# Survey loads on ACT's queue, a bias folded into a stored residual, and one unit's operand sums moved, in a one-layer encoder

## The chip, the cores and the metric

One core of a Trainium2 chip runs the whole kernel. Its engines are TensorE (PE, with PEld for weight loads), VectorE (DVE), ScalarE (ACT), GpSimd (POOL) and SyncE (SP); each runs its own instructions strictly in order, and instructions wait on semaphores. Transfers are carried out by 16 DMA engines and are started by an instruction in some engine's stream: here in SP's, but for one on POOL. Such an instruction can wait too, and everything behind it in the same stream then waits with it. The metric is device time in microseconds (us), median of several runs.

## The reference

A single post-norm encoder layer on x of 1024 tokens by 1024 features, float32, with 256 memory tokens. Cut to what matters:

```python
h = layer_norm(x, ln_in_w, ln_in_b)
h = layer_norm(ALPHA * h + hybrid_mixer(h, ...), ln1_w, ln1_b)        # mLSTM + neighbourhood attention, w_mix_out
h = layer_norm(ALPHA * h + memory_xattn(h, mem, w_xq, w_xkv, w_xo, b_xo), ln2_w, ln2_b)
h = layer_norm(ALPHA * h + conv_ffn(h, w_up, ..., w_down, b_down), ln3_w, ln3_b)

def memory_xattn(x, mem, w_q, w_kv, w_o, b_o):
    ...                                   # 4 heads of 256, softmax over 256 memory tokens
    return o @ w_o + b_o

def conv_ffn(x, w_up, b_up, w_dw, b_dw, w_down, b_down):
    h = x @ w_up + b_up                   # 1024 -> 2 * 2816
    h = depthwise_conv3(h, w_dw) + b_dw   # along the tokens
    g, u = split(h)
    return (gelu(g) * u) @ w_down + b_down
```

## The kernel before

Tokens are handled in eight tiles of 128 (`tt`). Each product is made from three matmuls (`mm3`, lines L217 to L219) of operands that were split into a high and a low part: a copy on ACT and a subtraction on DVE or POOL (`split`, `wload`, `split16`, L126/L127, L189/L190, L222/L223). The float16 splits need a power-of-two scale for each weight matrix, and that scale needs a bound on the matrix's entries. The **survey** finds it: `survey_gen` loads a matrix tile by tile into the buffers `sv` (two of them) and reduces each tile into one column of `sums`, on ACT by a sum of absolute values (L205) or, for column numbers in `BYMAX` (16 to 19), on DVE by a maximum (L203). `scale_of` later turns columns of `sums` into a scale. There are two surveys:

- the first, in the token-chunk stage: 11 tiles of `w_down`, 4 of `w_xo`, 4 of `w_xq` (1 MB each). Its next tile is asked for after a token chunk, inside `tc.issue_after(d.ins)`, which puts the load on SP behind that chunk's store `d` of the buffer `ev` (three buffers, L323 to L330);
- the second, in the stages of the mixer's output projection and of the cross-attention: 44 half-tiles of `w_up` (512 KB each), asked for in `after1` (one for each token tile) and in `attn` (one for each token tile, head and half), the rest by `run(survey)`. Its column numbers 16 to 19 fall into `BYMAX` too.

Stages, in order: input norm and token chunks (`tok_chunk`, PE tile `tk`, weight pieces of `w_tok`); column products (`cl`); mLSTM (`ml_gen`); neighbourhood attention (`na_gen`) with the output projection of the first half as filler; output projection of the second half (`out_half`), whose `after1` makes norm 1 (`ln_tile`), stores the normed tile `r` to the DRAM scratch `h1_d` (L930) and, three tiles later (`LAG`), transposes it into the float16 operands h1 (`to_T16`); query projection (`xq_gen`, PE tiles `xq` and `fill`); cross-attention (`attn`: scores `S`, softmax `P`, transposed `PT`, output `pv`) mixed with the query projection's second part and then with the cross output projection (`out_d`, PE tiles `od` and `out`); the feed-forward in 22 units (`Units`) of 128 columns; the down projection (`dn`).

`out_d` reads the residual back from `h1_d`: `load_r` (L1093) loads a tile into one of four buffers `r` and adds the bias row b_xo, already divided by ALPHA, on POOL (L1094). Norm 2 follows, with its statistics on DVE (L230 to L234), a power on POOL (L235), scale and shift on ACT, DVE and POOL (L241 to L243). Then `to_B` transposes the tile (PE, L989) and prepares the feed-forward's operands: even token tiles give B11 and B21, odd ones T1 to T4 and B22 (L998 to L1010).

A feed-forward unit `v` is one 128x2048 piece of `w_up` with four blocks A11, A12, A21, A22 in a buffer `ur` (two of them, loaded by `Units.load`, L1155). `Units.prep(v)` makes four sums S1 to S4 of the blocks on POOL (L1171 to L1174) into two buffers `wraw`, splits the A blocks from `ur`, then splits the S sums; it yields between these steps. `to_B` uses the same two `wraw` buffers for T1 to T4. Seven products `prod` make a unit: A11 with B11 and A12 with B21 come first and need no T operand; for units 0 and 1 they are issued before the loop over the units begins. `prep(0)` stands ahead of the last four tiles of `out_d`, `prep(1)` after nine steps of them (three tiles).

The written order is not the order on the engines. The program is traced as a whole, and an instruction scheduler with a simulated time line then chooses each engine's order: it starts what is ready when an engine is free, from far ahead in the program too. `mix` and `tc.issue_after` are the means by which the code holds something back: the instructions in such a block come after a named one on its engine.

Of the kernel before, what the change touches and what calls it, by code (L numbers as in the profile page):

```python
# [17 lines left out]
D = 1024  # L18
# [38 lines left out]
def encoder(ctx, tc, I, out):  # L57
# [134 lines left out]
    BYMAX = range(16, 20)  # L192

    def survey_gen(pool, src):

        for ap, i in src:
            shape = list(ap.shape)
            t = pool.tile(shape, F32, name="sv", tag="sv", bufs=2)
            S.dma_start(t, ap)
            if len(shape) > 2:  # L200
                t = t.rearrange("p a c -> p (a c)")
            if i in BYMAX:
                V.tensor_reduce(sums[:, i:i + 1], t, axis=mybir.AxisListType.X, op=OP.max, apply_absolute_value=True)  # L203
            else:
                A.activation(t, t, AF.Abs, accum_out=sums[:, i:i + 1])  # L205
            yield
# [61 lines left out]
    with ExitStack() as ca:  # L268

        yml = None  # L270
        with ExitStack() as cm:
# [19 lines left out]
            with ExitStack() as c1:  # L291
# [4 lines left out]
                    (I["w_xq"][2 * i:2 * i + 2].rearrange("i p k c -> p i (k c)"), 16 + i) for i in range(4)])  # L296
# [10 lines left out]
                def tok_chunk(c, tt, w):  # L307
# [13 lines left out]
                    else:  # L321
# [3 lines left out]
                        if c < 4:  # L325
                            d = S.dma_start(nv_d[tt * 128:(tt + 1) * 128, j:j + 256], e)
                        else:
                            A.activation(e, e, AF.Sigmoid)
                            G.tensor_tensor(e, e, mlw[:, j:j + 256], OP.mult)
                            d = S.dma_start(mo_d[tt * 128:(tt + 1) * 128, j:j + 256], e)  # L330
                        return d
# [33 lines left out]
                for c in range(2, 6):  # L365
                    w = [ws.get(2 * c), ws.get(2 * c + 1)]
                    for tt in range(NT):
                        d = tok_chunk(c, tt, w)
                        if tt % 2 == 0 or c > 3:
                            with tc.issue_after(d.ins):  # L370
                                next(survey, None)
# [521 lines left out]
    with ExitStack() as cb_:  # L893
# [12 lines left out]
        with ExitStack() as cB:  # L906
# [50 lines left out]
            for i in range(XQ0):  # L957
                if i > 0:
                    t_, r_ = rq.pop(0)
                    to_T16(r_, h1, t_, s1)  # L960
# [51 lines left out]
        with ExitStack() as cC:  # L1012
# [61 lines left out]
            bxo = vec(2, "b_xo")  # L1074
            V.tensor_scalar(bxo, bxo, 1.0 / ALPHA, None, op0=OP.mult)
# [14 lines left out]
            def load_r(tt):  # L1090
                if tt < NT:
                    rs[tt] = rt.tile([128, D], F32, name="r", tag="r", bufs=4)
                    S.dma_start(rs[tt], h1_d[tt * 128:(tt + 1) * 128, :])  # L1093
                    G.tensor_tensor(rs[tt], rs[tt], bxo, OP.add)  # L1094
# [51 lines left out]
        class Units:  # L1146
# [16 lines left out]
            def prep(self, v):  # L1163
# [4 lines left out]
                A21, A11, A12, A22 = (raw[:, i * 512:i * 512 + 512] for i in range(4))  # L1168
                s12, s34 = (wp.tile([128, WP], F32, name="wraw", tag="wraw", bufs=2)[:, :1024] for i in range(2))
# [6 lines left out]
                ah, sh_, al, sl = self.home(v)  # L1176
                k4 = lambda h, l, i: tuple(t[:, i * 512:i * 512 + 512].rearrange("p (k c) -> p k c", k=4) for t in (h, l))
                u = {"A11": k4(ah, al, 0), "A12": k4(ah, al, 1), "A22": k4(ah, al, 2)}
                for i in range(4):
                    u[f"S{i + 1}"] = k4(sh_, sl, i)  # L1180
                self.got[v] = u
                split16(ah, al, raw[:, 512:], su)
                yield
# [37 lines left out]
        with ExitStack() as cE:  # L1221
# [303 lines left out]
```

## Time and profile before

| | |
|---|---|
| time, median of 3 runs | 1627.49 us (1625.42 to 1632.18) |
| profiled execution | 1627.17 us, span 1625.5 us |
| mean granted TensorE clock | 0.969 |
| busy: PE, DVE, ACT, POOL | 1503.0, 973.4, 753.2, 544.6 us |
| moved by DMA | 226.69 MB, mean 139 GB/s |
| second survey's loads (`sv`<-`w_up`) | 44, from 636.1 to 796.6 us |

In the lines of the profile, L12 is line 12 of the kernel; an instruction is named engine, line, operation, tile written <- tiles read (buffer numbers left out), and its shape. In an order of time each row begins with the start and the duration in us; "[5.19 <-DVE ev L323]" says that the engine had been idle 5.19 us before it, and what released it. SPq is SP's stream of transfer issues; its rows with several issues ("x3") include waits between them. A row of the chain gives start, length and what was on the chain. A row of the waits gives who waited for whom, us in total, times, and the longest. Slices are 40 equal parts of the span, with digits for the busy share in tenths. PE's busy time is that of pipelined matmuls: whether PE is held up is read from its gaps and from the clock beside them.

### The profile page before, as it was taken

The numbers are of one execution on the slowest core, as the hardware profiler recorded it, in microseconds if no ns is written. First come the engines' busy times: TensorE is split into PE (matmuls) and PEld (weight loads), VectorE is DVE, ScalarE is ACT, GpSimd is POOL, SyncE is SP. The second block draws the span as 40 slices with busy tenths as digits, with TensorE's granted clock in tenths as the row PEclk, the third lists the DMA queues.
The fourth block names the chain that finished last, engine by engine and source line by source line (L and its number), as shares of the span: only waits on it lengthen the run. The fifth ranks groups of instructions, "written<-read, shape, count | busy, mean of one in ns | idle before, by whom it ended". The sixth has DMA issues, their size and how long they took to land.

```text
span 1625.5 us, 21513 instructions
## 1 busy us (share of the span) xinstructions
PE 1503.0 (92%) x8112; PEld 975.5 (60%) x8112; DVE 973.4 (60%) x1719; ACT 753.2 (46%) x1258; POOL 544.6 (34%) x372
## 2 busy tenths in 40 slices
PE   6998999999888989797789968999999999999997
PEld 5998888889777878644345533444444444444443
DVE  7411611237578885767566786887777676835333
ACT  3335201225555765656654444656665655622111
POOL 5414222114457761322002546454345410010133
PEclk9999999999999999898989978999999999999999
DMA  8278511266556325777631313222222232741112
GB/s 299 91 270 299 172 52 59 97 169 177 161 163 214 132 79 187 254 261 255 220 130 39 114 68 107 84 98 91 99 83 78 91 130 78 281 146 53 62 55 78
DMA packets 80377, 226.69 MB, mean 139 GB/s; under 512 B 7824, under 2 KB 26512, under 8 KB 76048
## 3 DMA queue, kind: packets, MB, share of 16 engines
q1 hardware_dynamic: 80128, 224.82, 40.3%
q8 instruction: 64, 1.05, 0.3%
q0 software_dynamic: 144, 0.49, 0.2%
q14 instruction: 41, 0.34, 0.1%
HBM read 182.71 MB, written 43.06 MB: 139 GB/s over the span
## 4 chain that ended last, share of the span: by engine, by line
PE 59%; DMA 12%; DVE 9%; ACT 6%; POOL 5%; issue 4%; SPq 0%; POOLq 0%; ACTq 0%; DVEq 0%
PE z L217 7%; PE z L218 7%; PE z L219 7%; PE dn L218 4%; PE dn L219 4%; PE dn L217 4%; DMA sv<-in_w_up_dram 4%; PE cl L217 4%; PE cl L219 4%; PE cl L218 4%; DMA whi<-mrow 2%; DMA mo<-ev 1%; ACT sv L205 1%; DMA r<-h 1%; PE o L863 1%
## 5 line engine op out<-in xcount | busy, mean ns | idle before, releaser
L127 POOL TENSOR_TENSOR wlo<-wraw,whi 128x1024 fp32r<-128x1024 f32 (+1 forms) x36 | 86.8, 2416 | 193.6 <-ACT whi L126 184.2
L190 DVE SCALAR_TENSOR_TENSOR wlo<-wraw,sc,whi 128x1024 f16<-128x1024 f32 x67 | 87.8, 1319 | 83.8 <-ACT whi L189 83.6
L217 PE MATMUL dn<-whi,yp 128*128 128x512 f16 x336 | 127.2, 379 | 0.0
L218 PE MATMUL dn<-wlo,yp 128*128 128x512 f16 x336 | 127.2, 379 | 0.0
L219 PE MATMUL dn<-whi,yp 128*128 128x512 f16 x336 | 126.9, 379 | 0.0
L189 ACT ACTIVATE whi<-wraw,sc 128x1024 f16<-128x1024 f32 x67 | 75.8, 1144 | 105.4 <-PE dn L219 46.3
L235 POOL TENSOR_TENSOR lnrs<-lnrs,mhalf 128x1 f32<-128x1 f32 x32 | 26.3, 822 | 283.9 <-DVE lnrs L234 161.6
L126 ACT ACTIVATE whi<-wraw 128x1024 fp32r<-128x1024 f32 (+1 forms) x48 | 50.4, 1056 | 121.8 <-PE cl L218 75.4
L205 ACT ACTIVATE sv<-sv 128x1024 f32<-128x1024 f32 (+1 forms) x55 | 70.9, 1289 | 71.8 <-DMA sv<-in_w_down_dram 38.3
L1173 POOL TENSOR_TENSOR wraw<-ur 128x512 f32<-128x512 f32 x22 | 41.2, 1873 | 156.1 <-DVE wlo L190 73.6
L243 POOL TENSOR_TENSOR r<-r,vec 128x1024 f32<-128x1024 f32 x22 | 51.8, 2356 | 77.5 <-DVE r L242 69.4
L1434 POOL TENSOR_TENSOR r<-r,vec 128x1024 f32<-128x1024 f32 x8 | 19.0, 2376 | 158.2 <-ACT r L1433 158.2
L1250 DVE SCALAR_TENSOR_TENSOR cbuf<-C,wdw,cbuf 128x1024 f32<-128x1024 f32 x44 | 70.7, 1607 | 1.1
L217 PEld LDWEIGHTS <-whi 128*128 128x128 f16 x364 | 36.3, 100 | 56.5 <-issue 16.5
L1249 DVE SCALAR_TENSOR_TENSOR cbuf<-C,wdw,cbuf 128x1024 f32<-128x1024 f32 x44 | 63.7, 1448 | 7.7 <-ACT cbuf L1248 6.7
L218 PEld LDWEIGHTS <-whi 128*128 128x128 f16 x364 | 36.2, 99 | 47.7 <-issue 7.7
L219 PEld LDWEIGHTS <-wlo 128*128 128x128 f16 x364 | 36.1, 99 | 45.1 <-issue 3.6
L217 PE MATMUL tk<-whi,X2h 128*128 128x256 f32 (+1 forms) x192 | 56.2, 292 | 6.5 <-DVE ev L323 5.2
L1248 ACT ACTIVATE cbuf<-C,bdw,wdw 128x1024 f32<-128x1024 f32 x44 | 54.4, 1236 | 12.2 <-DVE C L1286 11.4
L219 PEld LDWEIGHTS <-yp 128*128 128x128 f16 x352 | 34.4, 98 | 41.5
L217 PEld LDWEIGHTS <-yp 128*128 128x128 f16 x352 | 34.4, 98 | 41.5
L218 PEld LDWEIGHTS <-yp 128*128 128x128 f16 x352 | 34.4, 98 | 41.4
(444 smaller groups left out, 4850.9 us busy)
## 6 DMA issues: line engine op xcount, KB each, us to landing
sv<-in_w_up_dram SPq DMA_DIRECT2D x44, 512.0 KB
ur<-in_w_up_dram SPq DMA_DIRECT2D x22, 1024.0 KB
r<-h SPq DMA_DIRECT2D x23, 512.0 KB
sv<-in_w_down_dram SPq DMA_DIRECT2D x11, 1024.0 KB
y<-cbuf SPq DMA_DIRECT2D x22, 512.0 KB
ur<-y SPq DMA_DIRECT2D x11, 1024.0 KB
wraw<-in_w_down_dram SPq DMA_DIRECT2D x22, 512.0 KB
wraw<-in_w_col_dram SPq DMA_DIRECT2D x16, 512.0 KB
```

The source lines that it names most:

```text
L126: A.activation(hi[:, :n], r3, AF.Copy)
L127: (eng or G).tensor_tensor(lo[:, :n], r3, hi[:, :n].bitcast(F32), OP.subtract)
L189: A.activation(hi, src, AF.Copy, scale=s)
L190: V.scalar_tensor_tensor(lo, src, s, hi, op0=OP.mult, op1=OP.subtract)
L205: A.activation(t, t, AF.Abs, accum_out=sums[:, i:i + 1])
L217: T.matmul(ps, lh, rh, start=first, stop=False, skip_group_check=skip)
L218: T.matmul(ps, lh, rl, start=False, stop=False, skip_group_check=skip)
L219: return T.matmul(ps, ll, rh, start=False, stop=last, skip_group_check=skip)
L243: G.tensor_tensor(r, r, b_t, OP.add)
L1248: A.activation(c, C[:, 1:SEQ + 1], AF.Identity, scale=wdw[:, 1, j:j + 1], bias=bdw[:, j:j + 1])
L1249: V.scalar_tensor_tensor(c, C[:, 0:SEQ], wdw[:, 0, j:j + 1], c, op0=OP.mult, op1=OP.add)
L1250: V.scalar_tensor_tensor(c, C[:, 2:SEQ + 2], wdw[:, 2, j:j + 1], c, op0=OP.mult, op1=OP.add)
```

## The change

Three edits go together.

1. `survey_gen` issues its loads from ACT. It starts with two loads; then, for each tile, it makes the sum and issues the next load right behind it. The `issue_after` around the first survey is gone. Which columns are reduced on DVE is now an argument: 16 to 19 in the first survey, none in the second.
2. The bias b_xo is loaded before the output projection's second half. The new `to_h1` transposes a tile, then adds the bias in place on POOL, then stores it to `h1_d`; it takes the place of the transpose alone, three tiles behind the norm, and the earlier store is gone. `load_r` only loads, into one of five buffers.
3. `prep` gets the argument `early`, with which the split of the A blocks comes ahead of the S sums. Unit 1 is prepared that way: its A split after six steps of `out_d`, its S sums and their splits in the loop over the units. Unit 2 is loaded right behind `prep(0)`, and in the loop `units.load(v + 3)` comes after the sums of unit `v + 2`.

```diff
-    BYMAX = range(16, 20)
-    def survey_gen(pool, src):
-        for ap, i in src:
-            shape = list(ap.shape)
-            t = pool.tile(shape, F32, name="sv", tag="sv", bufs=2)
-            S.dma_start(t, ap)
...
-            if i in BYMAX:
+    def survey_gen(pool, src, bymax=()):
+        q = []
+        def load():
+            if src:
+                ap, i = src.pop(0)
+                t = pool.tile(list(ap.shape), F32, name="sv", tag="sv", bufs=2)
+                A.dma_start(t, ap)
+                q.append((t if len(ap.shape) == 2 else t.rearrange("p a c -> p (a c)"), i))
+        load()
+        load()
+        yield
+        while q:
+            t, i = q.pop(0)
+            if i in bymax:
                 V.tensor_reduce(sums[:, i:i + 1], t, axis=mybir.AxisListType.X, op=OP.max, apply_absolute_value=True)
             else:
                 A.activation(t, t, AF.Abs, accum_out=sums[:, i:i + 1])
+            load()
             yield
...
-                        d = tok_chunk(c, tt, w)
+                        tok_chunk(c, tt, w)
                         if tt % 2 == 0 or c > 3:
-                            with tc.issue_after(d.ins):
-                                next(survey, None)
+                            next(survey, None)
...
+            bxo = vec(2, "b_xo")
+            V.tensor_scalar(bxo, bxo, 1.0 / ALPHA, None, op0=OP.mult)
+            def to_h1(tt, r):
+                to_T16(r, h1, tt, s1)
+                G.tensor_tensor(r, r, bxo, OP.add)
+                S.dma_start(h1_d[tt * 128:(tt + 1) * 128, :], r)
             def after1(tt, r):
                 holds.append(ln_tile(r, lw, lb, small, hold=holds[-1] if holds else None))
-                S.dma_start(h1_d[tt * 128:(tt + 1) * 128, :], r)
                 next(survey, None)
                 rq.append((tt, r))
                 if len(rq) > LAG:
-                    t_, r_ = rq.pop(0)
-                    to_T16(r_, h1, t_, s1)
+                    to_h1(*rq.pop(0))
...
-                    rs[tt] = rt.tile([128, D], F32, name="r", tag="r", bufs=4)
+                    rs[tt] = rt.tile([128, D], F32, name="r", tag="r", bufs=5)
                     S.dma_start(rs[tt], h1_d[tt * 128:(tt + 1) * 128, :])
-                    G.tensor_tensor(rs[tt], rs[tt], bxo, OP.add)
...
+                if early:
+                    split16(ah, al, raw[:, 512:], su)
+                    yield
                 s12, s34 = (wp.tile([128, WP], F32, name="wraw", tag="wraw", bufs=2)[:, :1024] for i in range(2))
...
-                split16(ah, al, raw[:, 512:], su)
-                yield
+                if not early:
+                    split16(ah, al, raw[:, 512:], su)
+                    yield
...
         run(units.prep(0))
+        units.load(2)
         out_d2 = out_d(range(4, NT), "out", 1)
-        for _ in range(9):
+        for _ in range(6):
             next(out_d2)
-        run(units.prep(1))
-        units.load(2)
+        prep1 = units.prep(1, True)
+        next(prep1)
         run(out_d2)
...
             for v in range(NFF):
-                units.load(v + 3)
+                if v == 0:
+                    run(prep1)
                 pr = units.prep(v + 2)
                 next(pr, None)
+                units.load(v + 3)
```

More of the change, by code (lines that the diff above doesn't have):

```diff
@@ L190, in split16 @@
         V.scalar_tensor_tensor(lo, src, s, hi, op0=OP.mult, op1=OP.subtract)
-    BYMAX = range(16, 20)
-    def survey_gen(pool, src):
-        for ap, i in src:
-            shape = list(ap.shape)
-            t = pool.tile(shape, F32, name="sv", tag="sv", bufs=2)
-            S.dma_start(t, ap)
-            if len(shape) > 2:
-                t = t.rearrange("p a c -> p (a c)")
-            if i in BYMAX:
+    def survey_gen(pool, src, bymax=()):
[12 more added lines that the diff above has]
+            if i in bymax:
                 V.tensor_reduce(sums[:, i:i + 1], t, axis=mybir.AxisListType.X, op=OP.max, apply_absolute_value=True)
@@ L295, in encoder @@
                     (I["w_xo"][256 * i:256 * i + 256].rearrange("(a p) c -> p a c", a=2), 33 + i) for i in range(4)] + [
-                    (I["w_xq"][2 * i:2 * i + 2].rearrange("i p k c -> p i (k c)"), 16 + i) for i in range(4)])
+                    (I["w_xq"][2 * i:2 * i + 2].rearrange("i p k c -> p i (k c)"), 16 + i) for i in range(4)], range(16, 20))
                 ones = smallA.tile([128, 128], F32, name="ones")
@@ L325, in tok_chunk @@
                         if c < 4:
-                            d = S.dma_start(nv_d[tt * 128:(tt + 1) * 128, j:j + 256], e)
+                            S.dma_start(nv_d[tt * 128:(tt + 1) * 128, j:j + 256], e)
                         else:
@@ L329, in tok_chunk @@
                             G.tensor_tensor(e, e, mlw[:, j:j + 256], OP.mult)
-                            d = S.dma_start(mo_d[tt * 128:(tt + 1) * 128, j:j + 256], e)
-                        return d
+                            S.dma_start(mo_d[tt * 128:(tt + 1) * 128, j:j + 256], e)
                 xs = {}
@@ L958, in encoder @@
                 if i > 0:
-                    t_, r_ = rq.pop(0)
-                    to_T16(r_, h1, t_, s1)
+                    to_h1(*rq.pop(0))
                 next(xg)
@@ L1073, in encoder @@
             alx, epx = inx[:, 1:2], inx[:, 2:3]
-            bxo = vec(2, "b_xo")
-            V.tensor_scalar(bxo, bxo, 1.0 / ALPHA, None, op0=OP.mult)
             lw, lb = vec(0, "ln2_w"), vec(1, "ln2_b")
@@ L1161, in home, with prep @@
                 return homes[i]
-            def prep(self, v):
+            def prep(self, v, early=False):
                 if v >= NFF:
@@ L1168, in prep @@
                 A21, A11, A12, A22 = (raw[:, i * 512:i * 512 + 512] for i in range(4))
+                ah, sh_, al, sl = self.home(v)
+                k4 = lambda h, l, i: tuple(t[:, i * 512:i * 512 + 512].rearrange("p (k c) -> p k c", k=4) for t in (h, l))
+                u = {"A11": k4(ah, al, 0), "A12": k4(ah, al, 1), "A22": k4(ah, al, 2)}
+                for i in range(4):
+                    u[f"S{i + 1}"] = k4(sh_, sl, i)
+                self.got[v] = u
+                if early:
+                    split16(ah, al, raw[:, 512:], su)
+                    yield
                 s12, s34 = (wp.tile([128, WP], F32, name="wraw", tag="wraw", bufs=2)[:, :1024] for i in range(2))
@@ L1175, in prep @@
                 yield
[L1176 to L1181, printed above, removed]
-                split16(ah, al, raw[:, 512:], su)
-                yield
+                if not early:
+                    split16(ah, al, raw[:, 512:], su)
+                    yield
                 split16(sh_[:, :1024], sl[:, :1024], s12, su)
```

## The prediction

> **What bounds the kernel now.** I read the page's busy shares and slices first, then the table of stretches, then the chain and the waits, and went into the order of time only where TensorE (PE) idles. The table's columns are the stretch, its length, busy time (and count) of PE, PEld, DVE, ACT, POOL, then the granted clock, the DMA share and GB/s.
>
> ```profile
> PE 1503.0 (92%) x8112; PEld 975.5 (60%) x8112; DVE 973.4 (60%) x1719; ACT 753.2 (46%) x1258; POOL 544.6 (34%) x372
> PE   6998999999888989797789968999999999999997
> q1 hardware_dynamic: 80128, 224.82, 40.3%
> ...
> 0.00:40.00 40.00, 25.75 (x172) 23.18 (x173) 31.29 (x69) 14.47 (x17) 20.70 (x22) 1.00 0.82 304
> 156.00:164.00 8.00, 2.17 (x19) 1.75 (x17) 2.15 (x10) 2.74 (x5) 0.00 (x0) 0.75 0.98 324
> 164.00:180.00 16.00, 15.93 (x103) 15.32 (x104) 14.49 (x28) 3.89 (x7) 4.47 (x5) 0.81 0.73 248
> 640.00:840.00 200.00, 163.92 (x780) 95.75 (x779) 130.49 (x240) 122.60 (x213) 32.58 (x20) 0.90 0.69 237
> 955.00:1000.00 45.00, 25.09 (x90) 11.76 (x90) 36.40 (x40) 19.39 (x28) 26.00 (x23) 0.70 0.20 73
> 1000.00:1600.00 600.00, 598.95 (x2778) 271.82 (x2777) 388.30 (x364) 288.73 (x313) 182.44 (x96) 1.00 0.29 102
> ```
>
> From 1000 to 1600 us PE is full (598.95 of 600) at the full clock: nothing done there can show. The change can pay or cost only where PE has holes: the start, 156 to 180, 640 to 840 (36 us idle, clock 0.90), and 955 to 1000 (20 us idle, clock 0.70). The one dynamic hardware queue, q1, carries everything that SP issues; no row has a load issued by ACT.
>
> ```profile
> PE 59%; DMA 12%; DVE 9%; ACT 6%; POOL 5%; issue 4%; SPq 0%; POOLq 0%; ACTq 0%; DVEq 0%
> ...
> SPq L199 <- ACT sv L205: 71.4, 34, 7.1
> ...
> ACT sv L205 <- DMA sv<-in_w_up_dram: 27.1, 20, 3.7
> ```
>
> SP stood 71.4 us, 34 times, at the survey's load (L199) until ACT had summed the tile whose buffer it takes (L205); whatever SP had behind it stood too. ACT in turn stood 27.1 us for the survey's loads.
>
> **First survey (w_down, w_xo, w_xq).** Gain side:
>
> ```profile
> 154.63 2.64 SPq L330 DMA_DIRECT2D mo<-ev  x3
> 157.37 6.89 SPq L199 DMA_DIRECT2D sv<-in_w_xq_dram  x2
> ...
> 154.63 8.78 DMA mo<-ev
> ...
> 163.49 0.42 DVE L323 TENSOR_TENSOR ev<-tk,btok 128x256 f32<-128x256 f32 x1 [3.45 <-DMA mo<-ev]
> ...
> 163.97 0.58 PE L217 MATMUL tk<-whi,X2h 128*128 128x256 f32 x1 [5.19 <-DVE ev L323]
> ```
>
> A store of `ev` took 8.78 us among survey loads; DVE had no free `ev`, so PE had no free bank and idled 5.19 us. The stretch 156 to 164 lost 5.8 us and the next 16 us ran at 0.81 of the clock, 3.0 us more: 8.9 us. With the loads out of SP's queue the store no longer stands behind them. I take 9 gained; the ends are 0 (the store stays slow, because the DMA engines are 0.98 busy there) and 9.
>
> Cost side: the `issue_after` that held the loads behind SP's stores is gone. (The last row is from a tile's view: count, min/median/max ns, first and last start, forms.)
>
> ```profile
> 1.20 0.55 DVE L429 MEMSET cx<- 64x256 f32 x2
> ...
> 80.19 0.42 SPq L199 DMA_DIRECT2D sv<-in_w_down_dram  x1
> ...
> 10.71 1.11 ACT L126 ACTIVATE whi<-wraw 128x1088 fp32r<-128x1088 f32 x1 [8.62 <-DMA wraw<-in_w_tok_dram]
> ...
> L205 ACT ACTIVATE sv<-sv x55: 1043/1057/1918, 86.9 to 803.5; 128x1024 f32<-128x1024 f32 x40, 128x2048 f32<-128x2048 f32 x15
> ```
>
> The memset of `cx` is written far behind the token chunks and ran at 1.20 us: the order made for an engine takes whatever is ready. The first two survey loads wait for nothing, ACT has nothing else until 10.71, so I expect them at about 1 us instead of 80.19, with the sums following as tiles land. Two tiles are 2.1 MB, at the 304 GB/s of the first 40 us 6.9 us for whatever they delay, and there PE waits for x, the norm's vectors and the first weights. Two further tiles fit into the 18% of those 40 us in which the DMA engines are free. In pairs, 6.9 us to land and twice 1.9 us to sum, about 7 tiles come in 40 us: 24 us. I take 7 lost, near the lower end, since ACT's queue also holds evictions that wait for PE, and every such wait holds back the next survey load; ends 0 and 24.
>
> **Second survey (w_up, 44 tiles), 640 to 804 us.** The tile's view again, the chain, ACT and PE in order of time.
>
> ```profile
> L199 SPq DMA_DIRECT2D sv<-in_w_up_dram x44: 327/328/1167, 636.1 to 796.6; - x44
> L199 SPq DMA_DIRECT2D sv<-in_w_down_dram x11: 328/385/431, 80.2 to 138.7; - x11
> L203 DVE TENSOR_REDUCE sums<-sv x8: 1170/1743/2286, 168.6 to 713.3; 128x1 f32<-128x2048 f32 x4, 128x1 f32<-128x1024 f32 x4
> ...
> 768.97 5.49 DMA sv<-in_w_up_dram
> ...
> 774.54 1.06 ACT L205 ACTIVATE sv<-sv 128x1024 f32<-128x1024 f32 x1 [2.82 <-DMA sv<-in_w_up_dram]
> ...
> 778.48 0.59 PE L217 MATMUL pv<-PTh,vh 128*128 128x512 f16 x1 [5.36 <-ACT PTh L189]
> ```
>
> An issue on ACT has no row; the nearest is 0.33 us on SP. 44 of them are 14.5 us in ACT's queue, behind which stand its exponentials, splits and norms. The four tiles with numbers 16 to 19 also leave DVE (`bymax` is now empty here): 4.7 us off DVE, 4 x 1.06 = 4.2 us onto ACT. So ACT gets 19 us more in a stretch where it is busy 122.60 of 200. Cover: its 77 idle us; where the cover is gone (attention, whose softmax goes through ACT) up to 19 reach the path. For this SP's 71.4 us vanish, so w_xq, w_xo and K/V loads no longer queue behind sums; at best half of PE's 36 idle us, 18. But the hole at 778.48 stays: the load went at 768.97, as soon as its buffer was free, landed 5.49 us later, and ACT stood in order with the attention's copies behind it. Issuing it from ACT changes nothing there. The value between -18 and +19 I set at 0, because both rows are real and neither is nearer.
>
> Here the Trainium skill (DMA: Bandwidth & Descriptors) speaks on both sides. Its section "Issuing engines are not separate DMA queues" says that loads started by several engines run on the same 16 DMA engines, interleaved, and that a second issuer saves only issue time; by it both surveys gain nothing in transfer, which is the third rival below. Its section "Queues, rings and completion order" says that each issuer has a ring of its own and the engines alternate between rings packet by packet; by it the store at 154.63 would overtake the survey loads. No run here shows two rings yet.
>
> **Bias into the stored residual.**
>
> ```profile
> 951.01 2.35 POOL L1094 TENSOR_TENSOR r<-r,vec 128x1024 f32<-128x1024 f32 x1 [3.01 <-DMA r<-h]
> 953.31 0.55 POOL L235 TENSOR_TENSOR lnrs<-lnrs,mhalf 128x1 f32<-128x1 f32 x1
> ...
> 953.90 0.21 DVE L240 TENSOR_SCALAR lnrs<-lnmv,lnrs 128x1 f32<-128x1 f32 x1 [3.37 <-POOL lnrs L235]
> ...
> 959.12 1.12 PE L989 MATMUL tp<-ident,r 128*128 128x128 f32 x4 [3.98 <-POOL r L243]
> ```
>
> Eight adds on POOL leave the output projection for the stage before, and `load_r` gets a fifth buffer. On the path it is one add: DVE's statistics were out by 950.53 (953.90 - 3.37), POOL's power of them stood behind the add until 953.31, and PE's transposes wait for that norm. 953.31 - 950.53 = 2.8 us gained, ends 0 and 2.8. The eight adds (8 x 2.35 = 19 us) go to where POOL is busy 32.58 of 200 us; a norm's power may stand behind one there, up to 2.35 us once. The stores of h1, now after the transposes and the add, are read back one stage later. A tile of `r` comes free some 5 us later; with 7 buffers only the eighth load notices, up to 3 us. I cost these at 0. Loading b_xo earlier is one 512 KB load off the path.
>
> **Second unit's sums later.**
>
> ```profile
> 982.90 1.29 POOL L1174 TENSOR_TENSOR wraw<-ur,wraw 128x512 f32<-128x512 f32 x1
> ...
> 984.21 0.33 SPq L1155 DMA_DIRECT2D ur<-in_w_up_dram  x1
> ...
> 989.25 1.57 ACT L189 ACTIVATE whi<-ur,sc 128x1536 f16<-128x1536 f32 x1 [2.73 <-DMA ur<-in_w_up_dram]
> ...
> 986.80 0.38 PE L218 MATMUL z<-Bh,unitA 128*128 128x512 f16 x1
> 987.02 0.38 PE L219 MATMUL z<-Bh,unitA 128*128 128x512 f16 x1
> 991.91 0.38 PE L217 MATMUL z<-TX1l,unitYh 128*128 128x512 f16 x1 [4.51 <-ACT TX1l L1009]
> 994.29 0.58 PE L218 MATMUL z<-TX1l,unitYh 128*128 128x512 f16 x1 [1.78 <-DVE TX1l L1010]
> ...
> 999.36 0.50 PE L219 MATMUL z<-TX1l,wlo 128*128 128x512 f16 x1
> ```
>
> Unit 1's last sum (982.90) freed the raw buffer, SP loaded unit 3 into it at 984.21, and ACT had that unit's split in its order ahead of the last token tile's T operands: it idled 2.73 us for the load and spent 1.57 on the split. PE idled 4.51 and 1.78 us for those operands, and twelve products then ran at the low clock (994.29 to 999.36, 5.1 us, against 12 x 0.22 = 2.6 at the spacing of 986.80 and 987.02). In the new order these sums, unit 3's load and its split come behind the last tile, so ACT's 4.3 us leave the path and with the shorter hole most of the slow clock: 6.3 gained; ends 0 and 8.9 (both holes and the clock). Next late are the T operands' own copies and subtractions, some 2 us, and unit 1's S operands, which PE needs three products (36 matmuls, 7.9 us) later; if POOL's four sums (4 x 1.29 = 5.2 us) and the splits miss that, up to 4 us go back.
>
> **Sum.** First survey -9 + 7; second 0; bias -2.8; units -6.3: -11. The profiled execution took 1627.17 us (span 1625.5 and 1.7 around it), 0.3 below the median. 1627.2 - 11.1 = 1616.
>
> **Rivals.**
> Slower, from the start's transfers: survey rows are 8 KB, x and weight rows 4 KB. Row by row in turns, the survey takes two thirds while two loads are in flight, and 304 GB/s become 101 for SP. The 5.8 MB that PE's first chunks need (four x, two vectors, two weight halves, biases) then take 57 us instead of 19; less 0.8 MB of biases needed late (8 us), 30 us. 1627 - 18 + 30 = 1639. For it: ACT is free until 10.71 and DMA is already 0.82 busy. Against: ACT's order stops the survey whenever it waits. Slower than before from a start loss of 18 us on, clearly from 26.
> Better in the second survey: SP's freedom recovers 15 of the 36 idle us: 1601. For it: the 71.4 us. Against: the 5.49 us at 768.97.
> Transfers are the limit, not the queue: the `ev` store stays slow (share 0.98), so 9 is not gained and 7 is lost: 1627.2 - 9.1 + 7 = 1625. By the first of the two sections named above, this is the case.
>
> **How the numbers follow.** Forecast 1616, chance 0.45, its own range 1606 to 1623; start rival 0.22; second survey 0.13; transfers 0.20. What a measurement of this kernel tells from no change is about 0.5%, 8.1 us. Faster: 0.39 of the forecast, the 0.13, 0.02 of the last: 0.54. Same: 0.06, 0.15 and 0.02 of the start rival: 0.23. Slower: 0.20 and 0.03: 0.23. The range runs from below 1601 to above 1639: 1598 to 1642.
>
> **What would show it.** First survey: first ACT load near 1 us, PE's first transposes later than before, no hole near 158. Second: no SP wait on ACT's sums, ACT issues of about 0.33 us, idle sum of 640 to 840 about 36. Bias: no POOL add between statistics and power near 950. Units: no 4.51 us hole before the T products. Wrong if the first 80 us lose over 15 us, or if ACT's issues cost far more than 0.33.

## The result and the profile after

The changed kernel took 1642.14 us (median; 1638.92 to 1643.18) where the kernel before took 1629.27 beside it: ratio 1.0077, 95% interval 1.0049 to 1.0105. It is slower by 0.8%. The forecast was 1616; the first rival, a loss at the start, was put at 1639. The profiled execution took 1638.92 us, its span is 1637.2 and its mean clock 0.971.

From the page of the changed kernel, busy shares, PE's slices and DMA queues:

```profile
PE 1499.7 (92%) x8112; PEld 976.5 (60%) x8112; DVE 976.7 (60%) x1715; ACT 758.6 (46%) x1266; POOL 547.5 (33%) x372
PE   4989999999787998875889988899999999999997
q1 hardware_dynamic: 70032, 181.82, 32.6%
q10 hardware_dynamic: 10096, 43.00, 7.6%
```

Work and clock are about the same as before; PE's idle time is longer and lies in other places. The first slice fell from 6 to 4, and the weak slice at 158 is gone. A second queue, q10, has appeared: ACT's loads, 43 MB of 225. The table of stretches says where (columns as in the prediction):

```profile
0.00:40.00 40.00, 17.26 (x87) 15.13 (x88) 24.15 (x49) 19.12 (x23) 12.57 (x17) 0.94 0.96 372
...
80.00:156.00 76.00, 70.27 (x570) 69.57 (x569) 30.59 (x57) 20.34 (x23) 21.31 (x11) 0.98 0.55 184
156.00:180.00 24.00, 24.00 (x202) 24.00 (x202) 3.82 (x9) 5.54 (x11) 10.56 (x10) 1.00 0.29 94
...
640.00:840.00 200.00, 153.97 (x766) 95.38 (x765) 109.74 (x215) 119.11 (x212) 43.78 (x24) 0.90 0.67 229
...
955.00:1000.00 45.00, 35.02 (x160) 17.25 (x159) 35.56 (x47) 17.64 (x27) 21.18 (x11) 0.85 0.17 61
1000.00:1600.00 600.00, 592.30 (x2734) 267.99 (x2734) 409.29 (x368) 292.20 (x317) 195.40 (x110) 1.00 0.29 102
```

Five stretches changed. In the first 40 us the DMA engines moved more (372 GB/s against 304, share 0.96 against 0.82), and PE did half the matmuls (87 against 172): the wrong bytes came first. From 80 to 156 PE idles 5.7 us where it was full before (76.00 us, 634 matmuls). From 156 to 180 PE is now full at clock 1.00. From 640 to 840 PE idles 46 us instead of 36. From 955 to 1000 it idles 10 instead of 20, but the full stretch behind, which had 1 us of idle time, now has 8.

To put sizes to this, I compare when the same matmuls start, from the views of the tiles `tk`, `out`, `od` and `z` (in us, brackets: against the profile of before). The rows for the last matmul of the token chunks, of the kernel before, and then of the changed one:

```profile
L219 PE MATMUL tk<-whi,X2l x192: 274/283/415, 46.2 to 178.6; 128*128 128x256 f32 x160, 128*128 128x272 f32 x32
```

```profile
L226 PE MATMUL tk<-whi,X2l x192: 278/283/415, 59.4 to 190.5; 128*128 128x256 f32 x160, 128*128 128x272 f32 x32
```

| profile of | last token chunk | end of projection | last `od` | first product on T | last `z` |
|---|---|---|---|---|---|
| before | 178.6 | 678.3 | 912.4 | 991.9 | 1399.0 |
| changed | 190.5 (+11.9) | 689.7 (+11.4) | 930.2 (+17.8) | 999.5 (+7.6) | 1411.5 (+12.5) |
| everything held, e1 | 169.9 (-8.7) | 668.2 (-10.1) | 906.2 (-6.2) | 977.7 (-14.2) | 1389.7 (-9.3) |
| only first survey, e2 | 187.8 (+9.2) | 689.8 (+11.5) | 914.5 (+2.1) | 993.0 (+1.1) | 1400.1 (+1.1) |
| only second survey, e5 | 183.3 (+4.7) | 686.2 (+7.9) | 934.9 (+22.5) | 1014.2 (+22.3) | 1423.7 (+24.7) |
| only bias, e4 | 176.0 (-2.6) | 680.1 (+1.8) | 914.3 (+1.9) | 989.2 (-2.7) | 1396.2 (-2.8) |
| only units, e3 | 178.6 (0.0) | 680.9 (+2.6) | 915.4 (+3.0) | 990.4 (-1.5) | 1402.1 (+3.1) |
| pair free, e7 | 180.1 (+1.5) | 679.1 (+0.8) | 925.9 (+13.5) | 996.5 (+4.6) | 1408.4 (+9.4) |
| free in SP's queue, e10 | 175.9 (-2.7) | 674.5 (-3.8) | 911.3 (-1.1) | 990.6 (-1.3) | 1397.7 (-1.3) |
| held until 11.7, e13 | 175.2 (-3.4) | 678.6 (+0.3) | 917.1 (+4.7) | 987.2 (-4.7) | 1399.1 (+0.1) |
| k and v first, e12 | 170.9 (-7.7) | 669.0 (-9.3) | 901.5 (-10.9) | 969.3 (-22.6) | 1381.3 (-17.7) |

Stretches with the same code differ between profiles by up to about 3 us, once by 5 (e5's token stage, whose code is that of before), so single entries aren't read closer than that.

So the changed kernel stands as follows: 11.9 lost in the token stage (the hole at 158 gave back its 8.9, so the start lost 20.8), 5.9 more up to the last `od`, 10.2 gained up to the first product on T, 4.9 of that given back by the last `z`: +12.5.

**The start**, in order of time, of the kernel before:

```profile
10.79 1.97 PE L253 MATMUL tp<-ident,x 128*128 128x128 f32 x8 [10.79 <-DVE x L238]
...
13.17 3.29 SPq L125 DMA_DIRECT2D wraw<-in_w_tok_dram  x2
```

and of the changed kernel:

```profile
0.81 0.89 ACTq L200 DMA_DIRECT2D sv<-in_w_down_dram  x2
...
7.16 1.91 ACT L211 ACTIVATE sv<-sv 128x2048 f32<-128x2048 f32 x1
...
14.22 1.97 PE L260 MATMUL tp<-ident,x 128*128 128x128 f32 x8 [14.22 <-DVE x L245]
14.56 1.91 ACT L211 ACTIVATE sv<-sv 128x2048 f32<-128x2048 f32 x1 [5.40 <-DMA wraw<-in_w_tok_dram]
...
16.98 1.11 ACT L126 ACTIVATE whi<-wraw 128x1088 fp32r<-128x1088 f32 x1 [0.41 <-ACT sv L211]
...
19.44 3.08 SPq L125 DMA_DIRECT2D wraw<-in_w_tok_dram  x2
...
36.80 1.97 PE L260 MATMUL tp<-ident,x 128*128 128x128 f32 x8 [4.47 <-POOL x L250]
```

The first two survey loads went at 0.81, beside SP's first issues, and one had landed when ACT summed it at 7.16. PE's first transposes came at 14.22 instead of 10.79. ACT idled 5.40 us, by the profile for the first weight piece, but made the survey's second sum next and copied that piece only at 16.98 (10.71 before); so PE's first token-chunk matmul came at 18.6 instead of 12.6. The next weight loads went at 19.44 instead of 13.17, since their buffers came free later, and PE then stood 4.47 us for a tile of x.

Counting the token-chunk matmuls in order of their start, the changed kernel is 6.0 us behind at the first, 13.4 at the 49th (38 us), 15.6 at the 551st (112 us) and 22.2 at the 651st (130 us). So a delay of 3.4 us grew, but not by the opening alone: a third of the loss came near the end of the survey. DVE and PE, in order of time:

```profile
111.90 2.29 DVE L209 TENSOR_REDUCE sums<-sv 128x1 f32<-128x2048 f32 x1 [2.79 <-DMA sv<-in_w_xq_dram]
...
114.57 0.39 PE L224 MATMUL tk<-whi,X2h 128*128 128x256 f32 x1 [2.25 <-DVE ev L330]
```

DVE stood, in order, at its sums of the `w_xq` tiles, whose loads had not landed (2.83 us at the one before, 2.79 here); the copies to `ev` that free PE's banks stood behind them, and PE waited for DVE.

**Projection and attention**, in order of time, of the changed kernel:

```profile
693.11 1.06 ACT L211 ACTIVATE sv<-sv 128x1024 f32<-128x1024 f32 x1 [3.96 <-DMA sv<-in_w_up_dram]
...
694.17 1.13 ACT L189 ACTIVATE whi<-wraw,sc 128x1024 f16<-128x1024 f32 x1
...
695.34 1.28 DVE L190 SCALAR_TENSOR_TENSOR wlo<-wraw,sc,whi 128x1024 f16<-128x1024 f32 x1 [3.54 <-ACT whi L189]
...
702.67 1.94 PE L269 MATMUL tp<-ident,r 128*128 128x128 f32 x8 [11.68 <-DVE lnmv L239]
...
712.83 0.39 SPq L1030 DMA_DIRECT2D wraw<-xk  x1
...
747.51 1.06 ACT L211 ACTIVATE sv<-sv 128x1024 f32<-128x1024 f32 x1 [2.84 <-DMA sv<-in_w_up_dram]
...
750.79 1.06 ACT L211 ACTIVATE sv<-sv 128x1024 f32<-128x1024 f32 x1 [2.14 <-DMA sv<-in_w_up_dram]
...
758.98 1.06 ACT L211 ACTIVATE sv<-sv 128x1024 f32<-128x1024 f32 x1 [3.43 <-DMA sv<-in_w_up_dram]
...
760.60 0.72 ACT L189 ACTIVATE kh<-wraw,sc 128x512 f16<-128x512 f32 x1 [0.47 <-ACT sv L211]
...
761.37 0.80 PE L224 MATMUL S<-kh,pYh 128*128 128x256 f16 x3 [16.73 <-ACT kh L189]
```

This is how an in-order engine turns one late load into somebody else's hole. At 693.11 ACT had stood 3.96 us for a survey tile; the weight copy behind it came late, so DVE stood 3.54 us for that copy, and norm 1's statistics came late behind DVE's subtractions; PE stood 11.68 us. Later k was asked for at 712.83, but ACT copied it only at 760.60, behind sums that waited 2.84, 2.14 and 3.43 us for their loads, and PE stood 16.73 us. (This wait comes with the bias's edit, as e4 and e9 below show, not with the queue.) ACT's total for those loads, from the view of the waits, is 51.7 us in 31 waits (27.1 in 20 before):

```profile
ACT sv L211 <- DMA sv<-in_w_up_dram: 51.7, 31, 5.6
```

### The profile page after: what moved, and what is told of

The parts are those of the page before. It is cut to its first block, busy times and chain, and to the rows that moved or that the text cites. A ratio compares the mean times of both kernels' runs of the same rounds, so it can differ in the third digit from the quotient of the medians.

```text
span 1637.2 us, 21450 instructions
## 1 busy us (share of the span) xinstructions
PE 1499.7 (92%) x8112; PEld 976.5 (60%) x8112; DVE 976.7 (60%) x1715; ACT 758.6 (46%) x1266; POOL 547.5 (33%) x372
## 3 DMA queue, kind: packets, MB, share of 16 engines
q1 hardware_dynamic: 70032, 181.82, 32.6%
## 5 line engine op out<-in xcount | busy, mean ns | idle before, releaser
L190 DVE SCALAR_TENSOR_TENSOR wlo<-wraw,sc,whi 128x1024 f16<-128x1024 f32 x67 | 91.5, 1373 | 69.4 <-ACT whi L189 69.2
L242 POOL TENSOR_TENSOR lnrs<-lnrs,mhalf 128x1 f32<-128x1 f32 x32 | 25.0, 781 | 322.4 <-DVE lnrs L241 176.0
L211 ACT ACTIVATE sv<-sv 128x1024 f32<-128x1024 f32 (+1 forms) x59 | 75.2, 1275 | 61.6 <-DMA sv<-in_w_up_dram 51.7
L1189 POOL TENSOR_TENSOR wraw<-ur 128x512 f32<-128x512 f32 x22 | 32.0, 1453 | 150.7 <-DVE wlo L190 74.2
L1261 DVE SCALAR_TENSOR_TENSOR cbuf<-C,wdw,cbuf 128x1024 f32<-128x1024 f32 x44 | 74.7, 1698 | 11.8 <-ACT cbuf L1260 9.4
L1262 DVE SCALAR_TENSOR_TENSOR cbuf<-C,wdw,cbuf 128x1024 f32<-128x1024 f32 x44 | 72.0, 1636 | 1.2
L224 PE MATMUL tk<-whi,X1h 128*128 128x256 f32 (+1 forms) x192 | 57.5, 301 | 5.0 <-ACT X1h L229 2.7
L226 PEld LDWEIGHTS <-yp 128*128 128x128 f16 x352 | 34.4, 98 | 41.5
L225 PEld LDWEIGHTS <-yp 128*128 128x128 f16 x352 | 34.4, 98 | 41.4
```

What stands on the lines that cost most here:

```text
L190: V.scalar_tensor_tensor(lo, src, s, hi, op0=OP.mult, op1=OP.subtract)
L224: T.matmul(ps, lh, rh, start=first, stop=False, skip_group_check=skip)
L225: T.matmul(ps, lh, rl, start=False, stop=False, skip_group_check=skip)
L226: return T.matmul(ps, ll, rh, start=False, stop=last, skip_group_check=skip)
L1261: V.scalar_tensor_tensor(c, C[:, 0:SEQ], wdw[:, 0, j:j + 1], c, op0=OP.mult, op1=OP.add)
L1262: V.scalar_tensor_tensor(c, C[:, 2:SEQ + 2], wdw[:, 2, j:j + 1], c, op0=OP.mult, op1=OP.add)
```

## The experiments

All edits are on the kernel before or on the changed one. Ratios are to the kernel before, run beside them on the same chip. The theory: the start's survey loads make the loss. The rivals: the units, or the second survey on ACT.

### e1: the changed kernel with the first survey held back

```diff
     def split(hi, lo, src):
-        A.activation(hi, src, AF.Copy)
+        copied[0] = A.activation(hi, src, AF.Copy)
...
+                with tc.issue_after(copied[0].ins):
+                    next(survey, None)
                 for c in range(2, 6):
```

> The changed kernel with one thing put back: the first survey's two opening loads come on ACT behind the last copy of the transposed input (X2h), so that no survey load runs beside the input's and first weights' transfers. Theory A (the start's transfers): the last tk matmul, 178.6 us in before and 190.5 in the changed kernel, falls to 178.6 or, if the hole near 158 stays closed, to about 170; the time falls by 12 to 21 us from 1642, to 1621 to 1630. Theory B (the loss comes from ACT's issues and the second survey): the time stays within 4 us of 1642.

1619.95 us, ratio 0.9938 (0.9915 to 0.9960), against 1.0077 for the changed kernel. Tile view, last token-chunk row:

```profile
L227 PE MATMUL tk<-whi,X2l x192: 279/283/372, 46.0 to 169.9; 128*128 128x256 f32 x160, 128*128 128x272 f32 x32
```

190.5 - 169.9 = 20.6 us come back at that row, and 1.4% (23 us) in the time. The early loads cost the changed kernel more than its whole loss, and without them the change is faster than before.

### e2: the kernel before with only the first survey on ACT, not held

```diff
-                            with tc.issue_after(d.ins):
-                                next(survey, None)
+                            next(survey, None)      # and survey_gen of the change
```

> The kernel before with the first survey alone issued from ACT without the hold; second survey, bias and units as before. Theory A: the last tk near 190 us and about 12 us more than before, 1641. Theory B: within 3 us of before.

1629.12 us, ratio 0.9992 (0.9977 to 1.0006). The place was right (+9.2 at the last token chunk, +11.5 at the end of the projection), the total was not: in the attention, whose code is that of before, 9.4 us came back (+11.5 to +2.1). Which order of the engines made that, I did not find out. It is a warning that losses of stages don't simply add here: free loads at the start, without the other parts, leave the time as it was.

### e3: only the units

The diff is part 3 of the change. 

> The kernel before with the units' part alone (A split of unit 1 early, its S sums in the loop, unit 2 loaded behind prep(0)). Theory A (the hole before the T products closes, and S operands that come late give part of it back inside the first units): first z to T products about 5 us earlier, a new hole of 3 to 6 us between 1020 and 1045, in all 1 to 5 us faster than before. Theory B (nothing is given back, as the prediction's sum has it): 6 to 9 us faster.

1631.21 us, ratio 1.0005 (0.9993 to 1.0018): no change. In order of time, of this kernel:

```profile
992.02 0.38 PE L218 MATMUL z<-TX1l,unitYh 128*128 128x512 f16 x1 [1.27 <-DVE TX1l L1010]
...
1025.63 1.15 ACT L189 ACTIVATE unitYh<-wraw,sc 128x1024 f16<-128x1024 f32 x1 [2.69 <-POOL wraw L1183]
...
1027.82 0.67 ACT L1285 ACTIVATE vec<-z,bup 128x512 f32<-128x512 f32 x1
...
1028.54 0.38 PE L217 MATMUL z<-TX1h,unitA 128*128 128x512 f16 x1 [4.21 <-ACT vec L1285]
```

The holes of 4.51 and 1.78 us before the T products are now one of 1.27. But ACT's split of a unit's sums stands ahead of the copy that frees PE's bank, and waits 2.69 us for POOL: PE loses 4.21 us there. The changed kernel has the same hole.

### e4: only the bias

The diff is part 2 of the change. 

> The kernel before with the bias part alone (bias added and h1 stored behind the transposes, five buffers r in out_d). Theory A: POOL's power no longer waits near 950, about 3 us faster. Theory B: the eight adds on POOL and the later stores hold up the norms of the stage before (640 to 740), 2 to 8 us slower.

1625.28 us, ratio 0.9971 (0.9955 to 0.9987), 4.7 us less by the ratio. Its cost at norm 1, in order of time:

```profile
687.97 2.35 POOL L243 TENSOR_TENSOR r<-r,vec 128x1024 f32<-128x1024 f32 x1 [4.09 <-DVE r L242]
...
690.37 1.97 PE L262 MATMUL tp<-ident,r 128*128 128x128 f32 x8 [8.99 <-POOL r L243]
```

and from the waits of PE between 630 and 960 us:

```profile
PE S L217 <- ACT kh L189: 15.1, 2, 13.3
```

PE's wait at norm 1 is 8.99 us instead of 5.31, and the query projection begins 8 us later. PE also waits 15.1 us for ACT's split of k, 2.4 before. Still, the first `pv` matmul is only 3.4 late, and from the last `od` to the first T product the kernel gains 4.6.

### e5: only the second survey on ACT

```diff
-        survey = survey_gen(sv, [(I["w_up"]...
+        survey = survey_act(sv, [(I["w_up"]...      # the generator of the change
```

> The kernel before with one edit: only the second survey (w_up) is issued from ACT; the first one stays in SP's queue, bias and units as before. Theory A (it costs in the attention): ACT takes 44 issues of 0.33 us and stands for more loads, as in the changed kernel (51.7 us in 31 waits against 27.1 in 20), so from the projection's last matmul to the cross-attention's last filling matmul 3 to 6 us are lost, and the kernel is 0 to 8 us slower (ratio 1.000 to 1.005). Theory B (the shorter stretch of the kernel with only the first survey on ACT was chance, and SP's freedom from the sums is worth something): 5 us or more faster, with the sum of idle time of PE between 640 and 840 us below 30 us.

1650.05 us, ratio 1.0114 (1.0097 to 1.0131): 1.1% slower, more than theory A allowed. From the waits of PE between 640 and 960 us:

```profile
PE S L240 <- ACT P L1065: 14.3, 4, 7.7
PE tp L285 <- DVE lnrs L257: 9.8, 1, 9.8
```

The softmax's exponentials (6.3 us of waits before) and norm 1 (5.3 before) are late. In the changed kernel norm 1 is late too (11.7), the exponentials are not (3.1). From the end of the projection to the last `od` 14.6 us go (+7.9 to +22.5). Alone, this part costs as much as the change as a whole, or more (the intervals touch). So the second survey is a rival for the loss that e1 doesn't remove: with the start held its cost doesn't show (e9 below), but the changed kernel with the first survey left free and the second back in SP's queue was not run.

### e6: only the first survey, held

As e2, with the hold of e1. 

> The kernel before with only the first survey on ACT, its first load held behind the last copy of the first stage's input transposes. Theory A (the start's loads are the whole loss, the hole at 158 is a gain of 9 by itself): last token-chunk matmul at 170 us, 8 to 9 earlier than before, and 5 to 10 us faster in all. Rival (the gain of 10 us of the kernel with everything and the hold comes from bias and units): within 3 us of before.

1618.84 us, ratio 0.9920 (0.9905 to 0.9935): 0.8% faster by this alone (13 us by the ratio, more than expected). Moving the first survey forward, but behind the opening, closes the hole at 158, and no cost of it shows. Against e2 the hold is worth 0.7% here; in the changed kernel it was worth 1.4%.

### e7: the changed kernel with only the opening pair free

```diff
+                next(survey, None)
+                with tc.issue_after(copied[0].ins):
+                    next(survey, None)
+                    next(survey, None)
                 for c in range(2, 6):
```

> The changed kernel with only the opening pair of survey loads free; the sums and all later loads come behind the last copy of the first stage's input transposes. Theory A (each early tile takes its transfer time from SP's loads): the pair is 2.1 MB of the about 5 MB of survey tiles that came in the first 40 us, so it costs 7 us of the 21: last token-chunk matmul at 176 to 178 us, 13 us earlier than the changed kernel, time about 1627. Rival B (the sums in ACT's order, which stand for loads in front of the weight copies, make the loss, not the transfers): the pair costs under 3 us, last token-chunk matmul at 170 to 173 us, as with everything held, time about 1620 to 1623. Rival C (the pair alone makes most of it, because it stands ahead of everything): 185 us or later, time 1635 or more.

1635.02 us, ratio 1.0021 (1.0009 to 1.0033). PE's first transposes in order of time:

```profile
14.36 1.97 PE L261 MATMUL tp<-ident,x 128*128 128x128 f32 x8 [14.36 <-DVE x L246]
```

They are as late as in the changed kernel; the last token chunk is at 180.1, 10.2 us behind the held kernel and between the first and the last expectation. But these 10.2 aren't the pair's price at the opening. Counted as above, this kernel is 3 to 5 us behind the kernel before up to the 801st token-chunk matmul, less than the pair's transfer time of 6.9, and 11.8 behind at the 951st. The step lies at the survey's end again, DVE and PE in order of time:

```profile
131.34 0.16 DVE L173 TENSOR_REDUCE sc<-sums 128x1 f32<-128x4 f32 x1 [4.52 <-ACT sv L212]
...
135.24 0.58 PE L225 MATMUL tk<-whi,X1h 128*128 128x256 f32 x1 [2.78 <-DVE ev L331]
```

From 130 to 140 us the granted clock was 0.73 as well. The other 10.4 us of the changed kernel are the tiles behind the pair and ACT's sums ahead of the weight copies (here the first copy is at 14.24, there at 16.98); no run separates the two.

### e8: first survey held, and the bias

Second survey and units as before. 

> The kernel before with the first survey on ACT and held, and the bias edit; second survey in SP's queue and unit 1 prepared as before. Theory A (the gains of the first survey, about 9, and of the bias, 3 to 5, add): 1617 to 1619 us where the kernel before gives 1630, ratio 0.992 to 0.994, no worse than the changed kernel with the hold (1620). Rival (the stages behind swallow one of them, as in the kernel with only the first survey on ACT): under 6 us, ratio above 0.996.

1615.80 us, ratio 0.9899 (0.9884 to 0.9914): 0.2% below e6, with intervals that overlap. Whether the bias adds to the held survey is not settled by this.

### e9: the changed kernel with the hold, second survey as before

> The changed kernel with the hold, but with the second survey (w_up) back in SP's queue and its old generator: first survey on ACT and held, bias and units as changed. Theory A (the second survey on ACT is a loss by itself, seen in the traces as a longer wait for norm 1 and for the split of k): 4 to 8 us faster than the changed kernel with the hold (1620), so 1612 to 1616 where the kernel before gives 1630; idle of PE for the split of k under 3 us instead of 18. Rival (the second survey costs only where the start is late): 1619 to 1621.

1618.02 us, ratio 0.9923 (0.9909 to 0.9936), not to be told from e1's 0.9938. Theory A fell here: PE still waits 13.6 us for the split of k. That wait is in e4 too (15.1 us), where SP issues all loads. All kernels here with the bias's edit have it, at 11 to 20 us (but for e12 and e14, which change the order), and no kernel without that edit waits over 3.4, e5 included. So it doesn't hang on who issues the loads. Why the edit puts the split of k so far back in ACT's order, no run shows.

### e10: the kernel before with the hold taken away, loads still in SP's queue

The lines of e2's diff alone, with the old generator. 

> The kernel before with one thing taken away: the hold of the first survey's loads behind the stores; they stay in SP's queue. Theory A (what hurts the start is that the loads come through another queue, beside SP's): in one queue the first tiles stand behind x, the norm's vectors and the first weight pieces; first PE transpose as before (10.8 us), and the first 40 us as busy on PE as before (25 us). Later weight pieces still stand behind survey loads and SP's waits for the sums, so last token-chunk matmul between 170 and 182 us, time within 8 us of before. Rival (any survey tile that comes in the first 40 us costs its transfer time, whichever queue): about five tiles early, last token-chunk matmul 188 us or later, 10 us or more slower.

1628.74 us, ratio 0.9974 (0.9959 to 0.9989). Stretches:

```profile
0.00:40.00 40.00, 23.40 (x141) 21.44 (x142) 26.81 (x57) 18.52 (x22) 14.40 (x18) 0.96 0.96 370
```

and SP and PE in order of time:

```profile
10.08 1.68 SPq L199 DMA_DIRECT2D sv<-in_w_down_dram  x2
...
10.19 1.97 PE L253 MATMUL tp<-ident,x 128*128 128x128 f32 x8 [10.19 <-DVE x L238]
```

The same DMA share and rate in the first 40 us as in the changed kernel (0.96, 370 GB/s), and yet the last token chunk is 14.6 us earlier. So most of the loss isn't the bytes moved early, but which came first; 5 to 6 us remain against the held kernels (169.9 in e1, 170.7 in e6). In SP's own order the pair goes at 10.08, behind what PE needs. That left two explanations, the time of issue and the second queue.

### e13: the changed kernel, held only behind ACT's first weight copy

As e1, but anchored on the first `split` instead of the last. 

> The changed kernel with the first survey's loads held only behind ACT's first copy of a weight piece (10.7 us in the kernel before, first load expected at 12 to 14 us); from there they come as in the changed kernel, in ACT's own queue. Theory T (time of issue: only loads that come ahead of x, the norm's vectors and the first weight pieces cost): first PE transpose as before at 10.8 us, last token-chunk matmul at 171 to 177 us, as with free loads in SP's queue (175.9), time 1620 to 1627. Theory Q (the second queue: its loads share the engines with x tiles, weight pieces and stores for the first 80 us, whenever the first came): last token-chunk matmul at 182 us or later (190.5 in the changed kernel, 180.1 with the pair free), time 1632 or more.

1626.91 us, ratio 0.9971 (0.9956 to 0.9986). ACT and PE in order of time, and the stretch:

```profile
10.45 1.97 PE L262 MATMUL tp<-ident,x 128*128 128x128 f32 x8 [10.45 <-DVE x L247]
...
11.69 0.38 ACTq L201 DMA_DIRECT2D sv<-in_w_down_dram  x1
```

```profile
0.00:40.00 40.00, 23.70 (x130) 21.65 (x131) 27.68 (x56) 18.43 (x22) 15.81 (x19) 0.91 0.96 359
```

The loads are ACT's own again and free from 11.69 on; the last token chunk comes at 175.2, as with SP's queue (175.9). Theory T holds: what costs is that the loads, and ACT's sums of them, come ahead of the opening; the second queue by itself costs nothing that shows here. Free loads from 11.7 on still cost 5.3 us against e1.

### e11 and e14: the second survey by the new generator, issued from SP

```diff
-                A.dma_start(t, ap)
+                (E or A).dma_start(t, ap)           # E is S for w_up
```

On e1: 

> The changed kernel with the hold, with one thing changed: the second survey's loads are issued from SP, by the same new generator (sum, then next load, all 44 sums on ACT). Theory A (ACT's own issues are 44 x 0.33 = 15 us in its stream, and the wait for the k split is due to where the sums stand, not to who issues): 1617 to 1620, the hole at the first scores stays at 10 us or more. Rival (the issuing queue makes that hole): it goes below 4 us, 1612 to 1616.

1614.37 us, ratio 0.9893 (0.9878 to 0.9907), 0.45% below e1. The wait for the k split is 11.3 us and so stays, as theory A had it, but the time is better than it allowed.

On e12 (below): 

> The kernel with the attention's survey steps behind the split of k and v, with one thing changed: the second survey's loads are issued from SP. Theory A (issuing from ACT costs about 6 us of itself, as between the two kernels without the k and v order, 0.9938 and 0.9893): ratio to the kernel before 0.981 to 0.985 where it was 0.987. Rival (what issuing from ACT cost was the same wait in front of the k split, so it doesn't add): 0.986 to 0.989.

1615.70 us, ratio 0.9914 (0.9893 to 0.9935), slower than e12's 0.9873. Neither theory had that. Moving the same 44 issues to SP gained in one order and lost in the other, so no fixed price of ACT's queue can be given from these runs.

### e12: k and v split ahead of the survey's sums

On e1:

```diff
                 split16(t[2], t[3], vr, sv_)
+                copied[2] = copied[1]               # ACT's last copy in split16
...
-                        next(survey, None)
+                        with tc.issue_after(copied[2].ins):
+                            next(survey, None)
```

> The changed kernel with the hold, and the survey's steps that are written in the attention (sum and next load) put behind ACT's last split of the k and v operands loaded for it; nothing else changes. Theory A (the hole of 16 us in front of the first scores is ACT standing, in order, at survey sums whose loads have not landed, with the split of k behind them): idle of PE for that split falls from 18 us to under 4, first attention product 8 to 14 us earlier relative to the last query-projection matmul, and 4 to 12 us faster than the changed kernel with the hold (1620), unless the survey's end (w_up's scale) becomes late, which would show as idle time before the feed-forward's first product. Rival (the k split is late for its own data, or PE waits for something else there): hole of 10 us or more stays, time 1618 to 1622.

1610.75 us, ratio 0.9873 (0.9860 to 0.9887): the lowest of all, 1.3% below the kernel before and 2.0% below the changed one by the ratios; its interval lies below e1's and touches e11's. Waits of PE from 630 to 960 us, then ACT in order of time, then the tile's view:

```profile
PE S L225 <- ACT kh L190: 6.3, 1, 6.3
```

```profile
722.81 0.72 ACT L190 ACTIVATE kh<-wraw,sc 128x512 f16<-128x512 f32 x1 [4.54 <-DMA h<-r]
```

```profile
L201 ACTq DMA_DIRECT2D sv<-in_w_up_dram x44: 334/334/977, 632.7 to 898.0; - x44
```

k is copied at 722.81 instead of 740.02 in e1, PE's wait for it falls from 18.3 to 6.3 (under 4 was expected), and the first `pv` matmul comes at 733.9 instead of 754.1. The survey now ends at 898 instead of 790, under the output projection; some of the 20 us goes back there (-4.7 against e1 at the last `od`), but PE waits for nothing of it before the feed-forward (ACT stood 5.4 us for the scale).

## Why the prediction was wrong

**Start transfers, 7 us: the step that failed.** The mechanism was named (loads at about 1 us, seven tiles in 40 us; the trace has 0.81 and six), and so were the ends, 0 and 24. But I took 7, near the lower end, because ACT's order would stop the survey. It measured 20.8 in the profiles and 20.6 against the held kernel. The error was to price the pair by its transfer time and what follows from it at nothing. The pair alone put the stage 3 to 5 us back (e7), less than its 6.9. The rest came from order: ACT's sums stand ahead of the weight copies (16.98 for 10.71), each weight piece that is done with late frees its buffer late, so that the next load goes late (19.44 for 13.17), and near 112 us DVE stands at the `w_xq` tiles. How the 20.8 divide among these is read from the rows; beyond e7 no run takes them apart. The 304 GB/s said nothing on this, and e10 shows why: equal share and rate, another order, 5 to 6 us lost against the held kernels instead of 20.6. That the start rival named the outcome (1639) was luck, since both its terms were off: 30 for the start was too high (the loads that it lists come to 5.3 MB, not 5.8), and of its 18 gained elsewhere 8 were seen (8.9 + 10.2 - 4.9 - 5.9 = 8.3). The rival of a slow `ev` store fell, since 156 to 180 is full, and that of a better second survey fell with the idle sum, 46 us and not 21. ACT's stops, which I had counted as protection, came too late for the pair, which went ahead of the first of them; and ACT's order also worked the other way, by holding copies that PE needs behind the survey's sums.

The Trainium skill (DMA: Bandwidth & Descriptors, "Issuing engines are not separate DMA queues") says that all issuers' loads interleave on the same 16 engines. The trace agrees: from 6 to 8 us q10 and q1 moved 70 packets each, 0.57 and 0.29 MB, and SP's opening loads came 3.4 us late at PE. These are the two thirds that the start rival supposed, but q10 moved nothing from 10 to 14 us: the pair had landed.

**The hole at 158, -9.** Right in size: 156 to 180 is full at clock 1.00, where 5.8 us were idle and 3.0 slow. The reason was not shown: no store overtook a survey load, since the survey's last load now goes at 109.1 instead of 174.5. By which queue the store would have won, no run shows.

**Second survey, 0.** Wrong: alone it cost 14.6 us from the projection to the last `od` (e5), in the changed kernel 5.9 with the bias's adds (these make norm 1's wait 8.99 in e4). The issue time was right (0.334 us each). What I had listed and not priced was ACT standing in order at sums: 51.7 us for 27.1, of which either part alone makes about half (41.9 in e5, 39.6 with the bias alone in e4). In the kernel with the hold its share can't be told from nothing (e1 and e9).

**Bias, -2.8.** Right in sign: -4.7 (-2.1 to -7.3 by the interval). The wait of PE at norm 1 grew by 3.7 us, more than the 2.35 that I had named, and the one for the split of k, which I had not foreseen, by 12.7; alone, both were mostly absorbed. The second is there again as the hole of 16.73 us in the changed kernel.

**Units, -6.3.** The holes closed but for 1.28 us; up to 4 us were to come back and in the changed kernel 4.9 did, alone all of it. The place was another: ACT's copy of a product behind the split that waits for POOL. The changed kernel, in order of time:

```profile
1001.19 0.38 PE L225 MATMUL z<-TX1l,unitYh 128*128 128x512 f16 x1 [1.28 <-DVE TX1l L1020]
...
1037.87 0.38 PE L224 MATMUL z<-TX1h,unitA 128*128 128x512 f16 x1 [4.23 <-ACT vec L1292]
```

The first row is what is left of 4.51 and 1.78, the second is the new hole.

## What to carry to other kernels

A load that waits for nothing goes first if its issuing engine is idle at the start, so a background stream that moves to such a queue needs an explicit hold behind the work that opens the kernel. Price early loads by what they come ahead of, not by bandwidth. On an in-order engine, a step that waits for a background load belongs behind the copies that the bottleneck waits for: here that order was worth 0.65% (e1 to e12), and the queue about 0.4%, one way or the other (e11, e14).

## What was not expected of the hardware

With the same DMA share (0.96) and rate (370 and 372 GB/s) in the first 40 us, PE ran 141 matmuls in one kernel and 87 in another. A transfer issue by ACT took 0.334 us, by SP 0.328 (medians). Queue q10 moved its 43.00 MB at 7.6% of the engines' span, q1 181.82 MB at 32.6%: per MB the same within 2%, so no surcharge of the second queue shows.
